# Eight heads' softmax weights and three groups of q and k in the second layer: transposed by VectorE and transfers instead of TensorE

## The chip, the cores and the metric

One core of a Trainium2 chip runs the whole kernel in one launch. The metric is the device time of that launch in microseconds (us). The runs of the kernel before took 2664.18 to 2666.12 us.

## The reference, cut to what matters

Two transformer layers work on 256 tokens of width 2048, in float32. Each layer has two attention mixers, A and B, that share one input projection, and then a gated feed-forward with a short convolution. Only mixer B's attention and the q and k that lead to it are touched:

```python
qb = rmsnorm(qb.reshape(B, S, HB, HEAD_DIM), qn_b[l])
kb = rmsnorm(kb.reshape(B, S, HB, HEAD_DIM), kn_b[l])
...
s = jnp.einsum('brqhd,brikhd->bhrqik', qg, kg) * (HEAD_DIM ** -0.5)
s = jnp.where(col_mask[None, None, None, :, None, :], s + bias[None], NEG_INF)
p = jax.nn.softmax(s.reshape(B, HB, rows, GRID_W, kh * GRID_W), axis=-1)
o = jnp.einsum('bhrqik,brikhd->brqhd', p, vg)
```

There are 8 heads of width 128 in each mixer. With 256 tokens the window of B spans all grid rows, so a head's scores and weights are a full 256x256 matrix with a bias that also masks.

## The kernel before

**Weights.** All weight matrices are cut into 128x128 blocks, laid out in the order of use and loaded in units of 16 blocks (1 MB) by SyncE (SP) into one of four `raw` buffers, which the `aw` blocks of the conditioning vector share. ScalarE (ACT) casts half a unit to the rounded type (line 297) and VectorE (DVE) subtracts to get the remainder (line 298); four such split halves (`hl`) can lie ready. TensorE (PE) multiplies with the high and low parts in three passes (lines 314 to 316 with features as the output rows, 377 to 379 with tokens).

**Order of work.** A scheduler orders the instructions of each engine by program order and readiness; every engine then runs its own queue in order. After each unit of weights `Stream.tick` runs the background: functions put off with `bg.defer` run at the next tick, and generators registered with a rate are advanced by that many steps per tick. The attention of a layer is such a generator, `attention`: each step advances every live head by one `yield` and starts a new head if its groups of q, k and v are ready (`ready`). Its rate in the second layer is 0.4 per tick (`ATT[1]`) from the third group's projection on, and `ATT_B[1]` (0.21) after mixer A's output projection. What is left when the gate of B has been computed is run at once (`bg.finish(job)`).

**The second layer.** After 8 rows of gate A come nine groups of 512 columns of q, k and v in token layout, four units each. Group 0 holds A's k and v, 1 and 2 its q; 3, 4, 5 are k, v, q of B's heads 0 to 3 and 6, 7, 8 the same for heads 4 to 7. Then follow the rest of gate A, A's projection, gate B and B's projection, which needs all heads of B.

**Turning q and k.** `qk_rows` squares and sums a group on ACT, takes the power -0.5 on GpSimd (POOL, line 441), norms it on DVE three ticks later (line 556), and one tick after that `turn` transposes it, head by head: 8 transposes on PE into PSUM (`qtp`, line 580) and two scalings by ACT back to SBUF (line 581).

**A head.** First step: the bias load (line 825) and the split of q and k. Second: scores on PE (`sc`, line 607), sum with the bias and maximum on DVE (line 610), exponential and division on ACT (lines 618, 626). Third: four transposes of the weights `p` on PE (`tp`, line 631), and their split into high and low parts on ACT and DVE (`pT`, lines 389, 390). Fourth: product with v (`po`, line 639) and the split of the result (`oB`, lines 641, 642).

GpSimd issues no transfer; its only work at this place is the small power of each group.

Of the kernel before, what the change touches and what calls it, by code (L numbers as in the profile page):

```python
# [26 lines left out]
EPS = 1e-6  # L27
NEG = -1e30
SCALE = HEAD ** -0.5
GRID_W, NA_KH, NA_KW = 64, 8, 16  # L30


QKV_GROUPS = [1024, 0, 512, 2560, 3584, 1536, 3072, 4096, 2048]
# [45 lines left out]
H_RATE = [2.7, 1.7]  # L79

ATT = [1.288, 0.4]
ATT_B = [0.21, 0.21]

SCORES_3 = (1,)

ADA_ORDER = [[p * KC + k for k in range(KC) for p in ps] for ps in ((0, 1), (2,), (3, 4), (5,))]
ADA_ORDER = [i for part in ADA_ORDER for i in part]
# [47 lines left out]
def encoder(ctx: ExitStack, tc: tile.TileContext, a: dict, out: bass.AP):  # L135
# [16 lines left out]
    sm = pool("sm", 3)  # L152
    mm = pool("mm", 4, space=bass.MemoryType.PSUM)
    ax = pool("ax", 3, space=bass.MemoryType.PSUM)

    ident = const.tile([P, P], F32, name="ident")
    make_identity(nc, ident[:])
# [118 lines left out]
                pass  # L276

    bg = Paced()

    def unit_steps(l, u, by_halves=False):  # L280

        raw = rawp.tile([P, UB * P], F32, name=f"w{l}_{u}", tag="raw")
        if not by_halves:
            nc.sync.dma_start(raw[:], a["ws"][l, u])
        halves = []
        streamed = any(m == "w_in" and mo < GATE_A // P for m, _, mo in STREAMS[l][u * UB : (u + 1) * UB])
        at = OFF if streamed else 0
        for j in range(2):  # L290
            n = UB * P // 2
            hl = hlp.tile([P, 2 * n + ROW], F32R, name=f"hl{l}_{u}_{j}", tag="hl")
            hl = hl[:, at : at + 2 * n].rearrange("p (a n) -> p a n", a=2)
            r = raw[:, j * n : (j + 1) * n]
            if by_halves:
                nc.sync.dma_start(r, a["ws"][l, u][:, j * n : (j + 1) * n])
            nc.scalar.copy(hl[:, 0], r)  # L297
            nc.vector.tensor_tensor(out=hl[:, 1], in0=r, in1=hl[:, 0].bitcast(F32), op=ALU.subtract)  # L298
            halves.append(hl)
            if j == 0:  # L300
                yield halves
# [234 lines left out]
            nc.vector.tensor_tensor(out=z[:], in0=ps[:, :S], in1=self.rbs[:], op=ALU.mult)  # L536
            return z, sh

    def qk_rows(pss, heads, rot, gain, dst, then):

        cols = 0
        n = heads * HEAD
        ss = sm.tile([P, 8], F32, name="qss", tag="qss")
        for t, ps in enumerate(pss):
            for i in range(heads):
                sq = at.tile([P, HEAD], F32, name="qsq", tag="qsq", bufs=1)
                nc.scalar.activation(
                    out=sq[:], in_=ps[:, cols + i * HEAD : cols + (i + 1) * HEAD], func=AF.Square,
                    accum_out=ss[:, t * heads + i : t * heads + i + 1],
                )  # L550
        rs = sm.tile([P, 8], F32, name="qrs", tag="qrs")
        rsqrt(rs[:, : 2 * heads], ss[:, : 2 * heads], HEAD, 2 * heads)
        def norm():
            qn = at.tile([P, 2, 4, HEAD], F32, name="qn", tag="qn", bufs=1)
            for t, ps in enumerate(pss):
                nc.vector.tensor_tensor(
                    out=qn[:, t, :heads],
                    in0=ps[:, cols : cols + n].rearrange("p (h d) -> p h d", d=HEAD),
                    in1=rs[:, t * heads : (t + 1) * heads].unsqueeze(2).broadcast_to([P, heads, HEAD]),
                    op=ALU.mult,  # L560
                )
            if rot is not None:
                x1, x2 = qn[:, :, :heads, :HALF], qn[:, :, :heads, HALF:ROT]
                tab = [rot[:, i].unsqueeze(2).broadcast_to([P, 2, heads, HALF]) for i in range(4)]
                tm = []
                for i in range(2):
                    z = ev.tile([P, S], F32, name=f"rt{i}", tag="z")
                    z = z[:].rearrange("p (i t h d) -> p i t h d", i=2, t=2, h=4)
                    tm += [z[:, 0, :, :heads], z[:, 1, :, :heads]]
                for i, src in enumerate((x1, x2, x2, x1)):  # L570
                    nc.vector.tensor_tensor(out=tm[i], in0=src, in1=tab[i], op=ALU.mult)
                nc.vector.tensor_tensor(out=x1, in0=tm[0], in1=tm[1], op=ALU.subtract)
                nc.vector.tensor_tensor(out=x2, in0=tm[2], in1=tm[3], op=ALU.add)
            bg.defer(lambda: turn(qn))

        def turn(qn):
            for t in range(2):
                ps = ax.tile([P, 4, P], F32, name="qtp", tag="ax")
                for h in range(heads):
                    nc.tensor.transpose(ps[:, h], qn[:, t, h], ident[:])  # L580
                nc.scalar.activation(
                    out=dst[:, :, t * P : (t + 1) * P], in_=ps[:, :heads], func=AF.Identity, scale=gain
                )
            then()

        bg.defer(lambda: bg.defer(lambda: bg.defer(norm)))
# [12 lines left out]

        return ((0, 0), (0, 1), (1, 0))[: 2 * len(x) - 1]  # L600

    def attend(q, k, v, p, mask, scale, sink, o):

        sc = ax.tile([P, 2, S], F32, name="sc", tag="ax")
        for t in range(2):
            for i, j in by(q):
                nc.tensor.matmul(sc[:, t], q[i][:, t * P : (t + 1) * P], k[j], start=i + j == 0, stop=(i, j) == by(q)[-1])  # L607
        m = sm.tile([P, 2], F32, name="m", tag="m")
        for t in range(2):
            nc.vector.tensor_tensor_reduce(  # L610
                out=p[:, t], in0=sc[:, t], in1=mask[:, t], scale=scale, scalar=-3.0e38 if sink is None else sink,
                op0=ALU.add, op1=ALU.max, accum_out=m[:, t : t + 1],
            )
        nm = sm.tile([P, 2], F32, name="nm", tag="nm")
        nc.vector.tensor_scalar(out=nm[:], in0=m[:], scalar1=-1.0, scalar2=None, op0=ALU.mult)
        den = sm.tile([P, 2], F32, name="den", tag="den")
        for t in range(2):
            nc.scalar.activation(out=p[:, t], in_=p[:, t], func=AF.Exp, bias=nm[:, t : t + 1], accum_out=den[:, t : t + 1])
        if sink is not None:
            es = sm.tile([P, 2], F32, name="es", tag="es")  # L620
            nc.scalar.activation(out=es[:], in_=nm[:], func=AF.Exp, bias=sink)
            nc.vector.tensor_tensor(out=den[:], in0=den[:], in1=es[:], op=ALU.add)
        ri = sm.tile([P, 2], F32, name="ri", tag="ri")
        nc.vector.reciprocal(out=ri[:], in_=den[:])
        for t in range(2):
            nc.scalar.activation(out=p[:, t], in_=p[:, t], func=AF.Copy, scale=ri[:, t : t + 1])
        yield
        tp = ax.tile([P, 2, S], F32, name="tp", tag="ax")
        for k in range(2):
            for t in range(2):  # L630
                nc.tensor.transpose(tp[:, k, t * P : (t + 1) * P], p[:, t, k * P : (k + 1) * P], ident[:])  # L631
        pT = at.tile([P, 2, 2, S], F32R, name="pT", tag="pT", bufs=1)
        split(pT, tp[:])
        v = v()
        yield
        po = ax.tile([P, 512], F32, name="po", tag="ax")
        for i, j in by(v):
            for b in range(2):
                nc.tensor.matmul(po[:, :S], v[i][:, b], pT[:, j, b], start=i + j + b == 0, stop=i + b == 2)  # L639
        o = o()  # L640
        nc.scalar.copy(o[:, 0], po[:, :S])
        nc.vector.tensor_tensor(out=o[:, 1], in0=po[:, :S], in1=o[:, 0].bitcast(F32), op=ALU.subtract)
# [115 lines left out]
    for l in range(L):  # L758
# [35 lines left out]
        kTa, qTa = packs[0][:, 0:3:2], packs[0][:, 4:12]  # L794
        kvs = [None, None]

        ready, heads = [0], [0]
        oA, oB = [], []

        def head_a(i):  # L800
# [15 lines left out]
                    kvs[1] = in_halves(packs[0][:, 1:4:2, g * HEAD : (g + 1) * HEAD], f"vA{l}_{g}", "vh", True)  # L816
                return kvs[1]

            yield from attend(q, k, v, p, tables[0], SCALE, sink[:, i : i + 1], lambda: oA[i])

        def head_b(hb):
            b, i = packs[1 + hb // 4], hb % 4
            v = b[:, 4:8].rearrange("p (t a) s -> p t (a s)", t=2)
            p = at.tile([P, 2, S], F32, name="p", tag="p")
            nc.sync.dma_start(p[:], a["bias"][l, hb])
            q = in_halves(b[:, 8 + i], f"qB{l}_{hb}", "qh", l in SCORES_3)
            k = in_halves(b[:, i], f"kB{l}_{hb}", "kh", l in SCORES_3)
            yield
            yield from attend(
                q, k, lambda: in_halves(v[:, :, i * HEAD : (i + 1) * HEAD], f"vB{l}_{hb}", "vh", True), p, p, 1.0, None,  # L830
                lambda: oB_of(hb),
            )

        def oB_of(hb):
# [36 lines left out]
        for pi, (groups, gates) in enumerate(parts):  # L871
            last = pi == len(parts) - 1
            for g, part in enumerate(groups):
# [14 lines left out]
                    continue  # L888

                def turned(g=g):  # L890
                    ready[0] = g + 1

                vcol = {0: GA * HEAD, 4: 0, 7: 0}.get(g)
                if vcol is not None and pi == 0:
# [4 lines left out]
                elif g < 3:  # L899
                    qk_rows(pss, 4, rots[0], gains[:, 0:1], dst, turned)  # L900
                elif vcol is None:
                    qk_rows(pss, 4, None, gains[:, 3:4] if g in (3, 6) else gains[:, 2:3], dst, turned)
                else:
                    turned()
                if g == 2:
# [243 lines left out]
```

## Time and profile before

| what | value |
|---|---|
| runs, device time | 2666.12, 2664.18, 2664.96 us; median 2664.96 |
| profiled execution | span 2663.2 us from the first to the last instruction; the median of the runs lies 1.8 us above it |
| PE busy | 2650.9 us, 100% of the span |
| DVE, ACT, POOL busy | 2102.2, 1412.8, 36.2 us (79%, 53%, 1%) |
| moved | 700.41 MB, mean 263 GB/s |
| granted clock of TensorE | 1.000 |

How to read it: matmuls overlap in the pipeline, so busy time of PE says that it had work, not how fast it went; the chain of work shows what each instruction costs on the path. In the answers below PEld is TensorE's weight load, SPq the queue of SP, "<-" behind an instruction names what it reads, and "x8" counts instructions.

### The profile page before, as it was taken

To read this page: it belongs to the slowest core of one execution; us is meant where nothing else is said; L and a number is where in the kernel's file an instruction comes from. 1 tells how busy PE (TensorE), PEld (TensorE's weight loads), DVE (VectorE), ACT (ScalarE), POOL (GpSimd) and SP (SyncE) were. 2 spreads that over 40 slices of the span, in tenths; PEclk is the share of its full clock that TensorE was granted. 3 is DMA by queue.
4 is the path that set the end of the run, shared out by engine and by line. 5 is a ranking of instruction groups with operands and counts; after the bars stand their busy time and mean duration, and the time that the engine had idled before them with its cause. 6 is when DMAs were issued, how large, how long until landed. Compare 5 with 4: busy or idle time off the path is not lost.

```text
span 2663.2 us, 50845 instructions
## 1 busy us (share of the span) xinstructions
PE 2650.9 (100%) x21256; PEld 2565.7 (96%) x21256; DVE 2102.2 (79%) x2959; ACT 1412.8 (53%) x2284; POOL 36.2 (1%) x25
## 2 busy tenths in 40 slices
PE   9999999999999999999999999999999999999999
PEld 7888899999999999999998889999999999999999
DVE  8898998997987888788976667768888866655664
ACT  5445865456644555355555566554565445544553
POOL 0001100000000000000000000000000000000000
PEclk9999999999999999999999999999999999999999
DMA  9987789885787878788766666666747765555554
GB/s 372 351 327 292 262 300 352 317 320 199 291 294 287 302 288 295 289 294 289 290 217 254 228 229 231 245 252 253 285 173 288 297 256 190 190 194 194 197 191 143
DMA packets 102039, 700.41 MB, mean 263 GB/s; under 512 B 12721, under 2 KB 15025, under 8 KB 17969
## 3 DMA queue, kind: packets, MB, share of 16 engines
q1 hardware_dynamic: 101810, 697.17, 71.4%
q8 instruction: 166, 2.72, 0.4%
q14 instruction: 63, 0.52, 0.1%
HBM read 695.03 MB, written 2.10 MB: 262 GB/s over the span
## 4 chain that ended last, share of the span: by engine, by line
PE 89%; DVE 6%; ACT 1%; issue 1%; DMA 1%; POOL 0%; SPq 0%; DVEq 0%; ACTq 0%
PE ps L314 25%; PE ps L316 25%; PE ps L315 25%; PE ps_t L377 4%; PE ps_t L379 4%; PE ps_t L378 4%; DVE hl L298 2%; DVE aw L226 2%; DMA aw<-in_aw 1%; PE sc L607 1%; PE po L639 1%; ACT hl L297 1%; PE tp L631 1%; POOL qrs L441 0%; PE qtp L580 0%
## 5 line engine op out<-in xcount | busy, mean ns | idle before, releaser
L298 DVE TENSOR_TENSOR hl<-w,hl 128x1024 fp32r<-128x1024 f32 x928 | 1128.3, 1222 | 360.0 <-ACT hl L297 357.6
L297 ACT CAST hl<-w 128x1024 fp32r<-128x1024 f32 x928 | 970.7, 1049 | 748.5 <-PE ps L316 518.1
L314 PE MATMUL ps<-h,hl 128*128 128x256 f32 x3328 | 922.8, 277 | 1.3 <-DVE ya L915 0.6
L315 PE MATMUL ps<-h,hl 128*128 128x256 f32 x3328 | 919.8, 276 | 0.0
L316 PE MATMUL ps<-h,hl 128*128 128x256 f32 x3328 | 919.8, 277 | 0.0
L314 PEld LDWEIGHTS ps<-h,hl 128*128 128x128 f32 x3328 | 624.8, 188 | 2.4 <-DVE ya L915 0.8
L315 PEld LDWEIGHTS ps<-h,hl 128*128 128x128 f32 x3328 | 625.3, 188 | 0.4 <-DVE h L470 0.2
L316 PEld LDWEIGHTS ps<-h,hl 128*128 128x128 f32 x3328 | 624.4, 188 | 0.0
L226 DVE CUSTOM_DVE_ANT_0 aw<-aw,cact,ab 128x2048 f32<-128x2048 f32 x189 | 443.5, 2347 | 48.8 <-DMA aw<-in_aw 47.8
L377 PE MATMUL ps_t<-hl,h 128*128 128x512 f32 x576 | 223.1, 392 | 2.6 <-ACT h L469 2.1
L378 PE MATMUL ps_t<-hl,h 128*128 128x512 f32 x576 | 224.9, 391 | 0.3
L379 PE MATMUL ps_t<-hl,h 128*128 128x512 f32 x576 | 224.3, 390 | 0.0
L994 DVE SCALAR_TENSOR_TENSOR u<-ps,cw,u 128x255 f32<-128x255 f32 x304 | 146.1, 481 | 66.5 <-ACT u L992 62.2
L992 ACT ACTIVATE u<-ps,cw 128x256 f32<-128x256 f32 x152 | 85.9, 565 | 187.9 <-PE ps L316 187.5
L316 PE MATMUL ps<-merged,hl 128*128 128x256 f32 x512 | 141.8, 277 | 0.4 <-DVE hl L298 0.4
L315 PE MATMUL ps<-merged,hl 128*128 128x256 f32 x512 | 141.6, 277 | 0.0
L314 PE MATMUL ps<-merged,hl 128*128 128x256 f32 x512 | 141.6, 277 | 0.0
L315 PE MATMUL ps<-act_o,hl 128*128 128x256 f32 x512 | 141.4, 276 | 0.0
L316 PE MATMUL ps<-act_o,hl 128*128 128x256 f32 x512 | 141.3, 276 | 0.0
L314 PE MATMUL ps<-act_o,hl 128*128 128x256 f32 x512 | 141.2, 276 | 0.0
L377 PEld LDWEIGHTS ps_t<-hl,h 128*128 128x128 f32 x576 | 107.9, 188 | 26.1 <-ACT h L469 3.1
L378 PEld LDWEIGHTS ps_t<-hl,h 128*128 128x128 f32 x576 | 108.1, 188 | 23.7 <-DVE hl L298 1.9
(231 smaller groups left out, 4612.5 us busy)
## 6 DMA issues: line engine op xcount, KB each, us to landing
w<-in_ws SPq DMA_DIRECT2D x463, 1024.0 KB, 4.9
aw<-in_aw SPq DMA_DIRECT2D x189, 1024.0 KB, 6.1
p<-in_bias SPq DMA_DIRECT2D x16, 256.0 KB, 4.2
x<-in_xT SPq DMA_DIRECT2D x4, 512.0 KB, 5.3
aw_o<-in_aw SPq DMA_DIRECT2D x2, 1024.0 KB, 12.3
out<-x SPq DMA_DIRECT2D x16, 128.0 KB, 2.1
w<-in_ws SPq DMA_DIRECT2D x2, 512.0 KB, 11.7
aw_b<-in_aw SPq DMA_DIRECT2D x1, 1024.0 KB, 18.1
```

Of the source, the lines that this page charges most:

```text
L226: nc.vector.tensor_tensor_reduce(out=raw[:], in0=raw[:], in1=cact[:], scale=1.0, scalar=ab[:, i : i + 1], op0=ALU.mult, op1=ALU.add, accum ...
L297: nc.scalar.copy(hl[:, 0], r)
L298: nc.vector.tensor_tensor(out=hl[:, 1], in0=r, in1=hl[:, 0].bitcast(F32), op=ALU.subtract)
L314: nc.tensor.matmul(out, hi, act[0], start=first, stop=False)
L315: nc.tensor.matmul(ps[:, :S], hi, act[1], start=False, stop=False)
L316: nc.tensor.matmul(out, lo, act[0], start=False, stop=last)
L377: nc.tensor.matmul(ps[:], xh, hi, start=kc == kcs[0], stop=False)
L378: nc.tensor.matmul(ps[:], xh, lo, start=False, stop=False)
L379: nc.tensor.matmul(ps[:], xl, hi, start=False, stop=kc == kcs[-1])
L607: nc.tensor.matmul(sc[:, t], q[i][:, t * P : (t + 1) * P], k[j], start=i + j == 0, stop=(i, j) == by(q)[-1])
L992: nc.scalar.activation(out=u, in_=ps, func=AF.Identity, scale=w[:, 1:2], bias=w[:, 3:4])
L994: nc.vector.scalar_tensor_tensor(out=u[:, to], in0=ps[:, of], scalar=w[:, j : j + 1], in1=u[:, to], op0=ALU.mult, op1=ALU.add)
```

## The change

In the second layer all eight heads of mixer B and the groups 3, 5 and 6 no longer use PE to transpose. `turned_blocks` lets DVE transpose a 128-row tile in blocks of 32x32 (for a head, two tiles of 256 columns, written over that head's q and k, which have been split by then; for a group, two of 512 columns). GpSimd then sends each band of 32 rows to a scratch tensor in HBM, its 128-byte pieces put at the block's place in the transposed matrix: four transfers per tile, eight per head or group. SP reads the result back, for a head in two transfers four ticks later, for a group in one transfer seven ticks later; each read-back also waits for the latest subtraction of weights on DVE (`halved`). A group's scaling follows two ticks after its read-back, on SBUF data, and the group counts as ready then; since groups may now get ready out of order, `ready` counts only an unbroken run. A moved head takes two more steps, and the rate after A's projection is 0.4 instead of 0.21. Mixer A (`MOVED`'s first numbers) and the first layer keep the transposes of PE; `BACK`'s first entry serves heads of A and is not used.

```diff
-ATT_B = [0.21, 0.21]
+ATT_B = [0.21, 0.4]
...
+BACK = [3, 4]
+MOVED_QK = [(), (3, 5, 6)]
+BACK_QK = 7
+MOVED = [(0, 0), (0, 8)]
...
+    dram = pool("dram", 2, space=bass.MemoryType.DRAM)
...
+    def read_back(dst, src):
+
+        tc.add_manual_dep(nc.sync.dma_start(dst, src).ins, halved[0], BEHIND)
...
+    def later(n, fn):
+
+        if n == 0:
+            fn()
+        else:
+            bg.defer(lambda: later(n - 1, fn))
+
+    def turned_blocks(p, rows, n, tag):
+
+        y = dram.tile([P, n, S], F32, name=tag, tag=tag)
+        to = y[:].rearrange("(b i) n (t a j) -> t a i n b j", i=BLOCK, t=2, a=P // BLOCK)
+        for t, row in enumerate(rows):
+            nc.vector.transpose(out=row, in_=p[t])
+            src = row.rearrange("p (n b j) -> p n b j", n=n, j=BLOCK)
+            for a in range(P // BLOCK):
+                nc.gpsimd.dma_start(to[t, a], src[a * BLOCK : (a + 1) * BLOCK])
+        return y
...
+            halved[0] = nc.vector.tensor_tensor(
+                out=hl[:, 1], in0=r, in1=hl[:, 0].bitcast(F32), op=ALU.subtract
+            ).ins.name
...
         def turn(qn):
+            if moved:
+                rows = dst.rearrange("p (t a) s -> p t (a s)", t=2)
+                y = turned_blocks(
+                    [qn[:, t].rearrange("p h d -> p (h d)") for t in range(2)], [rows[:, t] for t in range(2)], heads, "qY"
+                )
+
+                def scaled():
+                    nc.scalar.activation(out=dst, in_=dst, func=AF.Identity, scale=gain)
+                    then()
+
+                later(BACK_QK, lambda: read_back(dst, y[:]))
+                later(BACK_QK + 2, scaled)
+                return
...
+        if rows is not None:
+            rows = rows()
+            y = turned_blocks([p[:, t] for t in range(2)], rows, 2, "pY")
+
+            def back():
+                for k in range(2):
+                    read_back(rows[k], y[:, k])
+
+            back = once(back)
+            later(BACK[sink is None], back)
+            yield
+            yield
+            back()
+            pT = at.tile([P, 2, 2, S], F32R, name="pT", tag="pT", bufs=1)
+            for k in range(2):
+                split(pT[:, :, k], rows[k])
+        else:
...
                 def turned(g=g):
-                    ready[0] = g + 1
+                    through.add(g)
+                    while ready[0] in through:
+                        ready[0] += 1
...
-                lambda: oB_of(hb),
+                lambda: oB_of(hb), (lambda: [b[:, 8 + i], b[:, i]]) if hb < MOVED[l][1] else None,
```

More of the change, by code (lines that the diff above doesn't have):

```diff
@@ L29 @@
 SCALE = HEAD ** -0.5
+BEHIND = mybir.DependencyInfo(mybir.DependencyClass.Sync, mybir.DependencyReason.DATA)
 GRID_W, NA_KH, NA_KW = 64, 8, 16
+BLOCK = 32
 QKV_GROUPS = [1024, 0, 512, 2560, 3584, 1536, 3072, 4096, 2048]
@@ L278, in encoder, with once, run @@
     bg = Paced()
+    halved = [None]
+    def once(fn):
+        due = [fn]
+        def run():
+            if due:
+                due.pop()()
+        return run
+    def read_back(dst, src):
[14 more added lines that the diff above has]
+        return y
     def unit_steps(l, u, by_halves=False):
@@ L297, in unit_steps @@
             nc.scalar.copy(hl[:, 0], r)
-            nc.vector.tensor_tensor(out=hl[:, 1], in0=r, in1=hl[:, 0].bitcast(F32), op=ALU.subtract)
+            halved[0] = nc.vector.tensor_tensor(
+                out=hl[:, 1], in0=r, in1=hl[:, 0].bitcast(F32), op=ALU.subtract
+            ).ins.name
             halves.append(hl)
@@ L537, in level, with qk_rows @@
             return z, sh
-    def qk_rows(pss, heads, rot, gain, dst, then):
+    def qk_rows(pss, heads, rot, gain, dst, then, moved=False):
         cols = 0
@@ L600, in by, with attend @@
         return ((0, 0), (0, 1), (1, 0))[: 2 * len(x) - 1]
-    def attend(q, k, v, p, mask, scale, sink, o):
+    def attend(q, k, v, p, mask, scale, sink, o, rows=None):
         sc = ax.tile([P, 2, S], F32, name="sc", tag="ax")
@@ L627, in attend @@
         yield
[L628 to L633, printed above, removed]
+        if rows is not None:
[13 more added lines that the diff above has]
+        else:
+            tp = ax.tile([P, 2, S], F32, name="tp", tag="ax")
+            for k in range(2):
+                for t in range(2):
+                    nc.tensor.transpose(tp[:, k, t * P : (t + 1) * P], p[:, t, k * P : (k + 1) * P], ident[:])
+            pT = at.tile([P, 2, 2, S], F32R, name="pT", tag="pT", bufs=1)
+            split(pT, tp[:])
         v = v()
@@ L795, in encoder @@
         kvs = [None, None]
-        ready, heads = [0], [0]
+        ready, heads, through = [0], [0], set()
         oA, oB = [], []
@@ L817, in v, with rows @@
                 return kvs[1]
-            yield from attend(q, k, v, p, tables[0], SCALE, sink[:, i : i + 1], lambda: oA[i])
+            def rows():
+                spare = ev.tile([P, S], F32, name=f"spare{l}_{i}", tag="r", bufs=2)
+                return [qTa[:, i], spare[:]]
+            yield from attend(
+                q, k, v, p, tables[0], SCALE, sink[:, i : i + 1], lambda: oA[i], rows if i < MOVED[l][0] else None
+            )
         def head_b(hb):
@@ L901, in encoder @@
                 elif vcol is None:
-                    qk_rows(pss, 4, None, gains[:, 3:4] if g in (3, 6) else gains[:, 2:3], dst, turned)
+                    qk_rows(pss, 4, None, gains[:, 3:4] if g in (3, 6) else gains[:, 2:3], dst, turned, g in MOVED_QK[l])
                 else:
```

## The prediction

> **What bounds the kernel now.** I read the page's totals first, then its chain of work, then the stage in question in 50 us windows.
>
> ```profile
> span 2663.2 us, 50845 instructions
> ...
> PE 2650.9 (100%) x21256; PEld 2565.7 (96%) x21256; DVE 2102.2 (79%) x2959; ACT 1412.8 (53%) x2284; POOL 36.2 (1%) x25
> ...
> PE 89%; DVE 6%; ACT 1%; issue 1%; DMA 1%; POOL 0%; SPq 0%; DVEq 0%; ACTq 0%
> ```
>
> TensorE carries 89% of the chain. The page is an average over the launch, so the windows (columns: length, then busy time of PE, PEld, DVE, ACT and POOL, clock, DMA share, GB/s) show the second layer's attention: up to about 1600 us the 512-column matmuls of q, k, v (245 in 50 us), then the 256-column ones of gates and projections (440).
>
> ```profile
> 1500.00:1550.00 50.00, 50.00 (x245) 42.10 (x244) 34.13 (x54) 32.00 (x65) 1.64 (x1) 1.00 0.63 229
> 1550.00:1600.00 50.00, 50.00 (x249) 42.26 (x248) 33.01 (x56) 31.61 (x70) 1.64 (x1) 1.00 0.62 231
> 1650.00:1700.00 50.00, 50.00 (x438) 50.00 (x438) 37.52 (x70) 28.27 (x52) 0.00 (x0) 1.00 0.64 235
> 1700.00:1750.00 50.00, 50.00 (x441) 50.00 (x440) 34.34 (x51) 28.10 (x53) 0.00 (x0) 1.00 0.65 242
> ...
> L607 PE MATMUL sc<-kB,qB x48: 276/276/369, 1633.8 to 1767.6; 128*128 128x256 f32 x48
> L631 PE MATMUL tp<-ident,p x128: 270/272/331, 281.1 to 1796.0; 128*128 128x128 f32 x128
> ```
>
> The last two rows, from the views of the tiles `sc` and `tp`, date the heads of B: first scores at 1633.8, last transposes at 1796.
>
> PE is busy throughout at clock 1.00. The view of waits, PE alone, from 1400 to 1830 us has one row:
>
> ```profile
> PE ps L315 <- DVE oB L642: 0.3, 1, 0.3
> ```
>
> So here each microsecond of PE work is one of wall time, DVE has 12 to 17 us free in 50, ACT 18 to 22, the transfer engines over a third, and POOL is nearly empty. Work taken from PE shortens this stage one for one, as long as its substitute never holds up the weights.
>
> **Removed: transposes on PE.** The chain in order of time (start, length) gives their price on the path.
>
> ```profile
> 1646.11 0.44 PE tp L631 x4
> ...
> 1694.92 0.70 PE po L639 x6
> 1695.62 0.44 PE tp L631 x4
> 1696.06 0.70 PE sc L607 x6
> ...
> 1556.48 0.87 PE qtp L580 x8
> ...
> 1581.04 0.87 PE qtp L580 x8
> ```
>
> Each head of mixer B loses four `tp`, 0.44 us; eight heads: 3.5 us. Groups 3, 5, 6 lose eight `qtp` each, 0.87 us; three groups: 2.6 us. Sum 6.1 us, which is 0.23% of 2663.2. That is the whole gain to be had here, because PE's waits in the stage add up to 0.3 us. Nothing in the first layer changes, and no other matmul goes; with those 0.3 the stage can give 6.4.
>
> **Added on DVE and ACT, under cover.** A transposition in blocks does not occur in the trace. Its nearest rows are elementwise operations of the same size:
>
> ```profile
> L390 DVE TENSOR_TENSOR pT<-tp,pT 128x512 fp32r<-128x512 f32 x16 | 10.9, 682 | 0.1
> L610 DVE CUSTOM_DVE_ANT_0 p<-sc,p 128x256 f32<-128x256 f32 x16 | 6.1, 418 | 0.0
> ...
> L581 ACT ACTIVATE packB<-qtp,gains x16: 667/690/696, 287.3 to 1633.1; 128x512 f32<-128x512 f32 x16
> ```
>
> DVE gains 16 of 128x256 at 0.42 us (6.7) and 6 of 128x512 at 0.68 (4.1); each `pT` split becomes two of 256 columns, 0.84 for 0.68, so 1.3 more over eight heads. Sum 12 us over the 250 us from 1545 to 1795, where the windows leave DVE at least 60 free. Even at four times the price a head's two blocks cost 3.4 us in a beat of 15 and fit. ACT trades two scalings of 512 columns (1.38 us) for one of 1024 (about the 1.05 of a weight cast below). I take nothing for these, covered by DVE's and ACT's idle time; bare of cover they would cost 12 us. Fewer gaps on DVE could also bring up to 0.3, the PE wait above.
>
> **Added on POOL: the unknown price.** Per head 2 x 4 transfers of 32 KB, cut into 256 pieces of 128 bytes; per group 8 of 64 KB in 512 pieces. That is 64 + 24 = 88 transfers. POOL issues none before, so the price `c` of one in POOL's queue must be bounded:
>
> ```profile
> 1562.91 1.64 POOL L441 TENSOR_TENSOR qrs<-qss,mhalf 128x8 f32<-128x8 f32 x1 [26.63 <-DVE qss L440]
> ...
> 1646.58 0.33 SPq L825 DMA_DIRECT2D p<-in_bias  x1
> 1648.07 0.33 SPq L286 DMA_DIRECT2D w<-in_ws  x1
> ...
> p<-in_bias SPq DMA_DIRECT2D x16, 256.0 KB, 4.2
> ```
>
> Low end 0.33 us, what SP needs to issue one. High end 4.2 us, the landing of the bias (256 rows of 1 KB, the same number of pieces), if every transfer had to wait for the one before. I take 1.64, POOL's time for a tiny instruction: the only row of that engine. It is nearest because eight transfers of a head are independent and may overlap.
>
> [...]
>
> **What c must not exceed.** The attention steps run at 0.4 per tick (one tick is one 1 MB unit of weights). These starts of `po` already stand at that rate, before the slower 0.21 sets in; with 1694.92 above, two beats:
>
> ```profile
> 1663.67 0.70 PE po L639 x6
> ...
> 1676.53 0.70 PE po L639 x6
> ```
>
> (1694.92 - 1663.67) / 2 = 15.6 us a head, 6.2 us a tick. At c = 1.64 a head's eight transfers take 13.1 us and POOL keeps up. The read-back is put off four ticks, 25 us. It stands in SP's queue, and every load of weights, `aw` and bias behind it waits with it. How long may it be late?
>
> ```profile
> L297 ACT CAST hl<-w x572: 1030/1050/1062, 16.8 to 1658.5; 128x1024 fp32r<-128x1024 f32 x191
> L286 SPq DMA_DIRECT2D w<-in_ws x287: 327/328/1261, 9.3 to 1648.1; - x144
> L296 SPq DMA_DIRECT2D w<-in_ws x2: 328/402/476, 5.3 to 9.0; - x2
> ...
> 1668.29 1.06 ACT L297 CAST hl<-w 128x1024 fp32r<-128x1024 f32 x1 [1.85 <-PE ps L316]
> 1689.44 1.06 ACT L297 CAST hl<-w 128x1024 fp32r<-128x1024 f32 x1 [1.70 <-PE ps L316]
> 1692.20 1.06 ACT L297 CAST hl<-w 128x1024 fp32r<-128x1024 f32 x1 [1.70 <-PE ps L316]
> ...
> w<-in_ws SPq DMA_DIRECT2D x463, 1024.0 KB, 4.9
> ...
> L298 DVE TENSOR_TENSOR hl<-w,hl 128x1024 fp32r<-128x1024 f32 x134 | 163.1, 1223 | 101.3 <-ACT hl L297 101.0
> ```
>
> Up to 1660 us SP has issued 287 units and one more in two halves, 288 in all, the last at 1648.07. The casts so far are 572 halves, so unit 288 is cast as number 575, the third after 1660, at 1668.29: 20.2 us after issue, 15.3 after a 4.9 us landing. Behind that four split halves lie ready, 2.76 us of PE each (1692.20 - 1689.44), less one cast and one subtraction (2.3): 8.7 us. PE thus notices a loading delay only after about 24 us.
>
> The eighth head's transfers end 64c after the first head's blocks; its read-back is due 7 x 15.6 + 25 = 134 us after them, and 24 more are hidden. POOL costs nothing up to c = 158 / 64 = 2.5 us. For the groups, 5 and 6 come closest, 24.6 us apart (1556.48 and 1581.04), with seven ticks, 43 us, of delay: 16c' = 24.6 + 43 + 24 gives c' = 5.7. Readiness comes nine ticks later, for group 5 at 1556.5 + 9 x 6.2 = 1612 and for group 6 at 1637; the first head of B starts its scores at 1634 and needs only groups 3 to 5, its fifth the rest.
>
> POOL's queue has another customer: each group's power `qrs`, and DVE stands still behind it.
>
> ```profile
> 1536.31 1.29 DVE L556 TENSOR_TENSOR qn<-ps_t,qrs 128x512 f32<-128x512 f32 x2 [1.81 <-POOL qrs L441]
> ```
>
> Group 5 is normed at 1536.3, its blocks can follow one tick later, 1542.5, and group 6's power comes at 1562.9: 20.4 us for eight transfers, so DVE waits from c' = 2.5 on, and behind it all halvings; PE has 8.7 us in hand, so it pays from c' = 3.6.
>
> **Added on the transfer engines and SP.** 64 x 256 + 24 x 512 = 28,700 short packets, 16 read-backs of 128 KB and three of 512 KB. The end of the kernel, where little but the 1 KB rows of `out` moves, bounds a short packet:
>
> ```profile
> 2640.00:2650.00 10.00, 10.00 (x90) 10.00 (x90) 4.86 (x7) 4.21 (x4) 0.00 (x0) 1.00 0.09 28
> ```
>
> 0.09 x 16 x 10 us over 273 packets is 53 ns. By bytes alone an eighth, 7 ns. So 12 to 95 us on each of 16 engines, spread over 250 us: share 0.64 becomes 0.69 to 1.0. I take a value near the low end, by bytes, and no loss; at the high end landings lengthen into the 24 us. 19 issues of 0.33 us cost SP nothing.
>
> **Sum.** 2663.2 - 6.1 = 2657.1 us of span. The median of 2664.96 lies 1.8 above the profiled span; that stays: 2658.9, forecast **2659.0**, if it holds 2657 to 2660.
>
> **Rivals.** (1) *The gain is eaten.* Group 6's power waits behind group 5's transfers, or a split waits some microseconds for its read-back behind 1 MB loads: PE loses 1 to 7 us, once or twice. At c' = 4, for instance, 32 - 20.4 - 8.7 = 3 us: 2662. For it: DVE already waits for POOL 1.8 us a group. Against: the slacks above.
>
> (2) *POOL becomes the bound, slower.* Place: SP's queue at the read-backs of the last heads. It decides from c = 2.5 us. At c = 3, which lies between my value and the high end, 64 x 3 - 158 = 34 us: 2693; at 4.2, 111 us: 2770. For it: transfers of many pieces written by an engine whose smallest instruction takes 1.64 us. Against: the same row, if pieces cost little.
>
> [...]
>
> **How the numbers follow.** Forecast 0.42, (1) 0.26, (2) 0.28, (3) 0.04. What a measurement can tell from no change is about 0.2%, 5.3 us: faster means below 2659.6, and the full gain clears that by less than 1 us. Faster 0.42, same 0.26, slower 0.32. The range starts at 2656.5, the forecast less the 0.3 of idle and 2 us for an altered order elsewhere, and goes to 2685, c = 2.9, leaving out (3) and about half of (2).
>
> **What would show it.** Right: PE loses 56 matmuls and the waits of PE stay under 1 us from 1500 to 1800; POOL shows under 2 us per transfer; casts of weights wait for PE, not for transfers. Wrong: casts `hl` waiting for `w`, read-backs on SP waiting long for POOL, DVE waiting for `qrs` over 9 us, or DVE's blocks costing far over 0.7 us.

## The result and the profile after

The changed kernel takes 2661.87 us (median of 18 runs, 2658.79 to 2665.32), the kernel before 2665.14 in the same comparison: ratio 0.9986, 95% interval 0.998 to 0.9993, so 1.9 to 5.3 us are saved, 3.7 by the ratio. The forecast was 6.1 us. The profiled run of the changed kernel has a span of 2661.6 us. Its page, totals, queues and chain:

```profile
span 2661.6 us, 50990 instructions
...
PE 2646.2 (99%) x21200; PEld 2560.0 (96%) x21200; DVE 2108.9 (79%) x2989; ACT 1411.9 (53%) x2289; POOL 94.4 (4%) x113
...
q0 software_dynamic: 2816, 3.68, 0.5%
...
PE 85%; DVE 7%; ACT 2%; DMA 2%; issue 2%; POOL 1%; SPq 0%; ACTq 0%; DVEq 0%; POOLq 0%
```

PE has exactly 56 matmuls fewer, POOL 88 instructions more, and a new queue, that of GpSimd's transfers, has appeared. Spans mix the change with the first layer, which varies from run to run (the second layer's first power starts at 1420.17 before and 1422.05 after, though nothing ahead of it differs). I therefore compare a stage: from that power to the power of the second layer's feed-forward norm. It holds all that was moved. First and last row of POOL's timeline (start, length), before, then after:

```profile
1420.17 1.05 POOL L441 TENSOR_TENSOR qrs<-qss,mhalf 128x4 f32<-128x4 f32 x1 [65.82 <-DVE qss L440]
...
1938.96 0.70 POOL L457 TENSOR_TENSOR nrs<-nss,mhalf 128x2 f32<-128x2 f32 x1 [323.97 <-DVE nss L519]
```

```profile
1422.05 1.05 POOL L484 TENSOR_TENSOR qrs<-qss,mhalf 128x4 f32<-128x4 f32 x1 [65.80 <-DVE qss L483]
...
1937.52 0.71 POOL L500 TENSOR_TENSOR nrs<-nss,mhalf 128x2 f32<-128x2 f32 x1 [180.69 <-DVE nss L562]
```

518.79 us became 515.47: 3.3 us less, about what the launch shows. The windows of the changed kernel and PE's waits from 1400 to 1830 us say where the rest went:

```profile
1550.00:1600.00 50.00, 48.43 (x235) 40.29 (x234) 36.08 (x60) 28.68 (x66) 9.91 (x13) 1.00 0.70 239
1600.00:1650.00 50.00, 48.76 (x392) 47.12 (x392) 34.04 (x59) 34.04 (x75) 6.83 (x9) 1.00 0.67 243
1650.00:1700.00 50.00, 50.00 (x439) 50.00 (x438) 39.95 (x80) 28.06 (x52) 14.71 (x24) 1.00 0.88 304
...
PE ps_t L421 <- DVE hl L339: 1.6, 1, 1.6
PE ps L359 <- DVE hl L339: 1.2, 1, 1.2
```

PE now stands still twice for a split half of weights, 2.8 us in all, and both times while groups of q and k are on their way, not while the heads are (1650 to 1700 is full). 6.1 - 2.8 = 3.3, which is what is missing. (The rate, measured below, is worth another 0.6 us that this sum leaves out, so it closes to about half a microsecond.) The first pause can be followed back through three engines, POOL first, then DVE, then PE:

```profile
1540.80 0.78 POOL L318 DMA_DIRECT2D qY<-packB  x1 [3.49 <-DVE packB L315]
1543.47 0.75 POOL L318 DMA_DIRECT2D qY<-packB  x1 [1.89 <-issue]
...
1564.10 0.74 POOL L318 DMA_DIRECT2D qY<-packB  x1 [3.69 <-issue]
1568.31 0.75 POOL L318 DMA_DIRECT2D qY<-packB  x1 [3.46 <-issue]
1569.07 1.67 POOL L484 TENSOR_TENSOR qrs<-qss,mhalf 128x8 f32<-128x8 f32 x1
...
1564.00 0.17 DVE L483 TENSOR_SCALAR qss<-qss 128x8 f32<-128x8 f32 x1
1570.77 1.29 DVE L599 TENSOR_TENSOR qn<-ps_t,qrs 128x512 f32<-128x512 f32 x2 [6.60 <-POOL qrs L484]
...
1573.11 1.30 DVE L315 STREAM_TRANSPOSE packB<-qn 128x512 f32<-128x512 f32 x2
1574.33 2.31 DVE L234 CUSTOM_DVE_ANT_0 aw<-aw,cact,ab 128x2048 f32<-128x2048 f32 x1
...
1576.57 1.22 DVE L339 TENSOR_TENSOR hl<-w,hl 128x1024 fp32r<-128x1024 f32 x1
...
1577.84 0.50 PE L421 MATMUL ps_t<-hl,h 128*128 128x512 f32 x1 [1.56 <-DVE hl L339]
```

Group 5's eight transfers take POOL from 1540.8 to 1569.1, 28.3 us, though each is only 0.75 us of work; between them POOL waits, mostly for something that the profile calls "issue". Group 6's sums are there at 1564.2, but its power stands behind the last transfer. DVE waits 6.6 us for it (1.8 before), and the halvings of weights stand behind it. DVE then does one halving, the group's blocks and an `aw` before the halving of 1576.57, and that is the one PE has run out for.

### The profile page after: what moved, and what is told of

The parts are those of the page before. It is cut to its first block, busy times and chain, and to the rows that moved or that the text cites. A ratio compares the mean times of both kernels' runs of the same rounds, so it can differ in the third digit from the quotient of the medians.

```text
span 2661.6 us, 50990 instructions
## 1 busy us (share of the span) xinstructions
PE 2646.2 (99%) x21200; PEld 2560.0 (96%) x21200; DVE 2108.9 (79%) x2989; ACT 1411.9 (53%) x2289; POOL 94.4 (4%) x113
## 3 DMA queue, kind: packets, MB, share of 16 engines
q0 software_dynamic: 2816, 3.68, 0.5%
## 4 chain that ended last, share of the span: by engine, by line
PE 85%; DVE 7%; ACT 2%; DMA 2%; issue 2%; POOL 1%; SPq 0%; ACTq 0%; DVEq 0%; POOLq 0%
PE ps L357 25%; PE ps L359 25%; PE ps L358 25%; PE ps_t L422 3%; PE ps_t L420 3%; PE ps_t L421 3%; DVE hl L339 3%; DVE aw L234 2%; DMA aw<-in_aw 2%; ACT hl L338 1%; PE sc L663 1%; PE po L712 1%; ACT qsq L590 0%; POOL qrs L484 0%; DMA packB<-qY 0%
```

## The experiments

**My theory.** The transposes taken off PE are worth 6.1 us; the loss comes from POOL's queue, where the transfers of a group are strung out because only so many of their pieces fit at a time into the scratch that GpSimd has for transfers (`dynamic_dma_scratch_size`, in bytes; not the scratch tensor in HBM); a second, smaller loss from the loads that stand behind group 6's read-back on SP. **Rivals:** the heads' traffic costs something; the transfers are slow to prepare; the read-backs hold up the weights.

**Parts alone.** Only heads: `MOVED_QK = [(), ()]`.

> Heads of mixer B moved as in the changed kernel, no groups of q and k moved. Stage = from the start of the second layer's first power qrs to the start of the power nrs of its feed-forward norm: 518.8 us before (1420.17 to 1938.96), 515.5 changed (1422.05 to 1937.52). Theory 1: the heads give their full 8 x 0.44 = 3.5 us and the 2.8 us lost on TensorE come from the groups alone: stage 515.3, no TensorE wait on hl between 1400 and 1830, launch about 3.5 us under before. Rival: the heads' transfers (DMA share 0.88 in 1650 to 1700 against 0.64) cost something too: stage 516.5 to 518.

Stage 514.55 (4.24 less, and 0.75 less than expected), no wait of PE at all, ratio 0.9978 (0.9969 to 0.9987). The heads give their share and lose nothing. Only groups: `MOVED = [(0, 0), (0, 0)]`, `ATT_B = [0.21, 0.21]`.

> Groups 3, 5 and 6 moved, no heads, the rate after A's projection back at 0.21. Theory 1: 2.6 us saved and 2.8 us lost in two waits of TensorE on hl (behind the power of group 6, and behind the aw load that stands behind group 6's read-back): stage 518.8 to 519, launch as before within 1 us. Rival: the losses need the heads as well: stage 516.2, launch 2.6 us under before.

Stage 518.49, just under what I expected, PE waits of 1.7 on `hl` and 0.3 on `oB` (the latter stood there before), ratio 0.9997 (0.9989 to 1.0006): moving the three groups at this scratch is worth nothing that can be measured. Here PE paid only at the second place; at the first, DVE waited 5.1 us and PE had just enough in hand. Only the rate: both lists empty, `ATT_B = [0.21, 0.4]`.

> Nothing is moved; only the rate of the attention after A's projection is 0.4 instead of 0.21. Theory 1: the rate brings at most the 0.3 us of TensorE's wait for oB: stage 518.4 to 518.8, launch as before. Rival (a part of the 4.2 us that the moved heads alone saved came from the rate): stage 517.5 to 518.2.

Stage 518.23, ratio 0.9998 (0.9989 to 1.0006). By this one profile the rate is worth 0.56 us in the stage, about twice the wait of 0.3 that I had named and at the edge of the rival's range; 4.24 - 0.56 = 3.7 remain for eight heads, against 3.5. Stages of single profiles fit such sums only to about half a microsecond, so the 0.56 is rough.

**The power behind the transfers.** Group 5 stays on PE: `MOVED_QK = [(), (3, 6)]`.

> As changed, but group 5 is left on TensorE, so that no power comes behind a group's transfers within 30 us. Theory 1: saves 3.5 + 2 x 0.87 = 5.2 us; VectorE's longest wait for qrs falls from 6.6 to 1.8 us, TensorE's wait of 1.6 us near 1578 is gone; the one of 1.2 us near 1634 may stay: stage 513.6 to 514.8. Rival (the loss belongs to the read-backs and to transfers in general, not to the power): stage 515.5 to 516.4, with 1 to 2 us of TensorE waits left.

Stage 513.50, DVE's longest wait for `qrs` 1.8 us, PE's pause near 1578 gone and 0.5 us left at the second place; ratio 0.9981 (0.9972 to 0.999). It saves less PE work than the changed kernel, yet its stage is 2 us shorter than in the profile above. Two more profiles with group 5 moved, below, have 513.64 and 513.95, so most of those 2 us is spread between runs; what this run shows is that DVE's long wait and PE's first pause go with group 5's transfers.

**Room for pieces.** More scratch, with 512 bytes freed elsewhere; the order of instructions on every engine is that of the changed kernel:

```diff
-    nc = _bacc.Bacc("TRN2", target_bir_lowering=False, num_devices=1, dynamic_dma_scratch_size=1024)
+    nc = _bacc.Bacc("TRN2", target_bir_lowering=False, num_devices=1, dynamic_dma_scratch_size=1536)
...
-                sq = at.tile([P, HEAD], F32, name="qsq", tag="qsq", bufs=1)
+                sq = ev.tile([P, HEAD], F32, name="qsq", tag="sqa", bufs=1)
```

> As changed, with 1536 instead of 1024 bytes of scratch for GpSimd's transfers; the 512 bytes come from the squares' junk output, which now lies in another buffer. The order of instructions is the same. Theory 1: POOL's pauses between transfers (2 to 5.5 us between two of a group, three of a head in a row and then a pause) are waits for room for their pieces: two of a group and five of a head fit now, a group's eight take under 20 us instead of 28, VectorE's longest wait for qrs falls from 6.6 to about 2 us, and TensorE's wait behind it is gone: stage 513.9. Rival: the pauses are the time of preparing the pieces: a group keeps 28 us, stage 515.5.

> The kernel with 1536 bytes of scratch once more. Theory 1: stage 512.5 to 513.2, TensorE's waits under 0.7 us, launch 1 to 3 us under the changed kernel in the same comparison, about 6 us under before. Rival (its first result was the chip's): no difference to the changed kernel.

Stages 512.77 and 512.78, PE waits 0.6 and 0.8, ratios 0.9971 (0.996 to 0.9983) and 0.997 (0.9959 to 0.9981). The stages are 1.1 us below the 513.9 that I expected of the first; the 0.8 lies just above my 0.7. POOL's timeline of the first of these runs, with group 5 and the first head:

```profile
1538.02 1.52 POOL L318 DMA_DIRECT2D qY<-packB  x2 [3.49 <-DVE packB L315]
1540.70 1.51 POOL L318 DMA_DIRECT2D qY<-packB  x2 [1.16 <-issue]
...
1551.66 0.74 POOL L318 DMA_DIRECT2D qY<-packB  x1 [2.69 <-issue]
1561.31 1.67 POOL L484 TENSOR_TENSOR qrs<-qss,mhalf 128x8 f32<-128x8 f32 x1 [8.91 <-DVE qss L483]
...
1637.65 3.06 POOL L318 DMA_DIRECT2D pY<-packB  x5 [26.25 <-DVE packB L315]
1640.96 1.82 POOL L318 DMA_DIRECT2D pY<-packB  x3 [0.25 <-issue]
```

Two of a group go at once instead of one, five of a head instead of three; the eight are through in 14.4 us (1538.02 to 1552.40), and POOL is idle when the power comes. The same first head with 1024 and with 768 bytes:

```profile
1643.14 1.86 POOL L318 DMA_DIRECT2D pY<-packB  x3 [25.39 <-DVE packB L315]
1646.82 1.86 POOL L318 DMA_DIRECT2D pY<-packB  x3 [1.82 <-issue]
```

```profile
1644.04 1.26 POOL L318 DMA_DIRECT2D pY<-packB  x2 [26.50 <-DVE packB L315]
1646.99 1.23 POOL L318 DMA_DIRECT2D pY<-packB  x2 [1.69 <-issue]
```

With 256 pieces a transfer, 2, 3 and 5 in a row at 768, 1024 and 1536 bytes, and one or two of 512 pieces at 1024 and 1536: the pieces under way stay below the number of bytes, and one transfer more would reach it. Counted over the whole of the changed kernel, from each issue to its landing, the pieces under way peak at 768; with 768 bytes no row of transfers is longer than two, 512 pieces. And in the changed kernel each of group 5's transfers starts 0.3 us after the one before has landed, whether that took 2.3 or 5.5 us. That is room as the limit, and not the preparing. Two controls. Only the output of the squares that nobody reads (`qsq`, the junk output) moved as above, scratch 1024:

> As changed with scratch at 1024, and only the squares' junk output moved to the other buffer as in the run with more scratch. Theory 1: the move does nothing by itself; stage 515 to 516, VectorE's longest wait for qrs near 6.6 us, POOL's group chains 28 us. Rival (the gain of that run came from the other place of the buffers): stage 512.8, launch as in that run.

Launch ratio 0.9988 (0.9979 to 0.9997), as the changed kernel, and DVE's wait for `qrs` still 5.0 us. The stage of the profiled run was 513.64, lower than I expected of it. And the changed kernel again:

> The changed kernel once more, beside the next one. Theory 1: the launch lies about 3 us under before; in the profiled run TensorE's waits on hl between 1400 and 1830 add up to 1 to 3 us and the stage is 512.5 plus these waits, 513.5 to 515.5. Rival (the profiled run of the changed kernel was an odd one): waits under 0.5 us and a launch 6 us under before.

Ratio 0.9984 (0.9975 to 0.9992); stage 513.95 with 1.8 us of PE waits. So the profiled run of the changed kernel was on the high side, by 1.5 us. With DVE at the edge, how long POOL's transfers take to land decides from run to run whether PE notices: group 5's eight took 28.3 us there, 26.8 in the repeat and with the junk output moved, 26.4 with the groups alone; DVE then waited 6.6, 5.2, 5.0 and 5.1 us, and PE's first pause was 1.6, 0.4, 0.5 and none. The three profiles with all moved and 1024 bytes have stages of 513.6 to 515.5, the two with 1536 both 512.8. The launches' intervals overlap, so the gain of scratch on the launch, some 2 to 4 us, is likely rather than proven.

A way without more scratch: each transfer of a group in two of 16 rows.

```diff
-                nc.gpsimd.dma_start(to[t, a], src[a * BLOCK : (a + 1) * BLOCK])
+                step = 2 * BLOCK // n
+                for i in range(0, BLOCK, step):
+                    nc.gpsimd.dma_start(to[t, a][i : i + step], src[a * BLOCK + i : a * BLOCK + i + step])
```

> As changed, scratch at 1024, but each transfer of a group goes in two of 16 rows: 16 transfers of 256 pieces instead of 8 of 512, like those of the heads. Theory 1 (POOL waits for room for pieces): three of the small ones fit where one large one did, so that one and a half times as much is under way: a group's chain falls from 28 to about 19 us, VectorE's longest wait for qrs to about 2 us, stage 513 to 513.9. Rival (each transfer costs POOL a fixed time of preparation): 16 transfers take longer than 8, over 28 us, VectorE's wait grows beyond 6.6 us, stage 516 to 518.

Stage 513.05, group 5's sixteen transfers through in 19.6 us (1542.63 to 1562.23), DVE's longest wait for `qrs` 1.9, PE's waits 1.0, ratio 0.9978 (0.9969 to 0.9987). Twice as many transfers are faster, which speaks against a price per transfer.

**Less room.** `dynamic_dma_scratch_size=768`, the same order of instructions.

> As changed, with 768 bytes of scratch instead of 1024: two transfers of a head fit at a time instead of three, one of a group as before. Theory 1 (room for pieces sets POOL's pace): a head's eight transfers take about 17 us at 4.3 us of landing each, over the 15.6 of a beat, POOL falls behind from head to head, SP's waits for pY at the read-backs rise from 4 us to 10 us and more, and the stage grows by 0 to 5 us to 515 to 520. Rival (POOL has room to spare): SP's waits and the stage stay as in the changed kernel, 513.5 to 515.5.

Slower: ratio 1.0012 (1.0004 to 1.0021), stage 521.74, more than I allowed. Waits of this kernel, SP, DVE, PE:

```profile
SPq L301 <- DMA pY<-packB: 56.7, 23, 7.2
...
DVE aw L234 <- DMA aw<-in_aw: 38.0, 13, 6.5
...
PE ps L359 <- DVE hl L339: 7.0, 6, 3.5
```

This is rival (2) of the prediction, at its place: the read-backs wait on SP for POOL, the loads behind them are late, and PE pays: some 6 of the 7.0 us fall between 1728 and 1798, where the heads' read-backs are. The 64 transfers of the heads ran from 1644.04 to 1780.88, 2.1 us each with all pauses (the changed kernel: 114 us, 1.8).

**No extra wait at the read-back.** `read_back` without the dependence on `halved`, only `nc.sync.dma_start(dst, src)`.

> As changed, but the read-backs no longer wait for the latest subtraction on VectorE; in SP's order they stand one to three loads earlier. Theory 1: SP then waits for POOL's transfers at the read-backs (now 5.5 us in all), by 20 us and more in all, hidden up to about 24 us each: TensorE loses 0 to 5 us more, stage 515.5 to 520. Rival (the extra wait itself holds back the loads of aw behind it, and is what costs 1.2 us near 1634): stage 513 to 515.

Far worse than either theory: ratio 1.0144 (1.013 to 1.0158), stage 557.2. With nothing to hold them back, the scheduler's order lets SP come to the read-backs, and ACT to the scalings that use them, long before POOL's transfers have landed. SP waits 123 us at them; what PE feels is ACT's row, 44.0 us, because ACT's casts of weights queue behind it:

```profile
SPq L301 <- DMA pY<-packB: 71.1, 26, 9.4
...
SPq L301 <- DMA qY<-packB: 52.0, 11, 12.2
...
ACT packB L627 <- DMA packB<-qY: 44.0, 3, 16.2
...
PE ps_t L420 <- ACT hl L338: 22.2, 3, 9.3
```

Three windows of the same run (the last three numbers of a row are the granted clock, the DMA share and GB/s):

```profile
1570.00:1580.00 10.00, 6.55 (x37) 5.56 (x35) 0.00 (x0) 0.00 (x0) 2.23 (x3) 0.97 0.14 21
1580.00:1590.00 10.00, 3.68 (x8) 2.62 (x9) 2.31 (x4) 6.47 (x15) 1.67 (x1) 0.52 0.41 158
1590.00:1600.00 10.00, 7.49 (x33) 5.75 (x32) 10.00 (x17) 3.09 (x8) 1.53 (x2) 1.00 0.59 205
```

PE stood still for 9.3 us, into the second window; the eight matmuls behind the pause share 3.68 us of busy time there, 0.46 each, at a granted clock of 0.52, the 33 of the third window 7.49, 0.23 each, at 1.00. So this pause cost more than itself. Shorter pauses were not alike: the third window has 2.5 us without work for PE, and the ten us behind it show 0.83, while the run with 768 bytes, whose longest wait of PE for a split half was 3.5 us, has a mean clock of 1.000 (this run 0.993). The pauses of 1.6 and 1.2 us in the changed kernel lie in windows of 1.00.

**More of the same.** The kernel with 1536 bytes and six heads of mixer A moved as well, `MOVED = [(0, 0), (6, 8)]`.

> As the run with 1536 bytes of scratch (stage 512.8), with the softmax weights of the first six heads of mixer A in the second layer moved as well. Theory 1: each head more takes 0.44 to 0.53 us off TensorE: 2.6 to 3.2 us, stage 509.6 to 510.2, if POOL gets through three groups at 14 us and six heads at 10 us, about 100 us of work in the 115 us from 1495 to 1610. Rival: the powers now stand behind the heads' transfers, VectorE waits for qrs over 10 us at a time and the halvings behind it come late: stage 513 to 518.

The rival came, and by far more than its 513 to 518: ratio 1.0042 (1.003 to 1.0055), stage 529.6. Among PE's waits are 6.5 us for a split half and 5.4 for the softmax weights of a head that stayed on PE; DVE's row shows why:

```profile
1573.68 1.29 DVE L599 TENSOR_TENSOR qn<-ps_t,qrs 128x512 f32<-128x512 f32 x2 [11.47 <-POOL qrs L484]
```

POOL had groups and heads at once, and the power stood behind both. PE's pauses of 6.5 and 5.4 us lie in the windows 1550 to 1600 and 1600 to 1650, whose granted clock was 0.93 each, against 1.00 in those before and behind, which adds to the loss.

## Why the prediction was right, and where it was not

*What is saved* held: 6.1 us. The heads gave 3.7; the groups 0.3 net of 1.7 us of new waits; with enough scratch the stage fell by 6.0 with under 1 us of waits left, the rate's 0.56 included.

*DVE's and the transfer engines' part* held: after the change the blocks are one row each,

```profile
L315 DVE STREAM_TRANSPOSE packB<-p 128x256 f32<-128x256 f32 x16 | 6.4, 430 | 1.7 <-ACT p L682 1.7
L315 DVE STREAM_TRANSPOSE packB<-qn 128x512 f32<-128x512 f32 x6 | 3.9, 687 | 0.0
```

6.4 and 3.9 us against 6.7 and 4.1. The new queue holds 0.5% of 16 engines' span, 13 us each, at the low end of 12 to 95; it records 32 packets a transfer, as many as a band has rows, not 256 or 512.

*POOL's price* was the mis-sized term. I took 1.64 us for both kinds. The heads cost about 1.1 us each when POOL had one head (8.5 us for the first eight) and 1.8 over all; a group's transfer costs 28.3 / 8 = 3.5 us. Only one of 512 pieces was under way, so each paid its landing, 2.3 to 5.5 us in group 5. That no row before showed a limit on what POOL may have under way is why I bounded `c` by 4.2 but took a value that assumed overlap. The 1.64 was also read badly: I called it the only row of POOL and its smallest instruction, but the 0.70 and 1.05 us shown above stood in the same trace, and the instruction of a transfer takes 0.61 or 0.75. The price was the wait between transfers, which no row of a POOL instruction could give.

*The queue behind POOL* was named with its place: 8c' - 20.4 gives a wait of 7.6 us at 3.5, and 6.6 was measured, of which 1.7 is the power itself. But I let PE pay only from c' = 3.6, with 8.7 us in hand; it paid 1.6 us at 3.5, and in the other profiles it began to pay at a DVE wait of about 5 us. The 8.7 took off only one cast and one subtraction, and put the rest that DVE has to do between two halvings, here the norm, the blocks and an `aw` (1.29 + 1.30 + 2.31 us), at nothing. So the likeliest case, no loss, did not come; rival (1) did. That it said 2662 and 2661.9 was measured is partly luck: its 3 us were one pause at c' = 4, and the 2.8 here are two pauses at 3.5, the second from another cause. And a range from 2656.5 to 2685 would have held most outcomes.

*The slack* of 24 us was too generous, as the run with 768 bytes shows: at 136.8 us for the 64 transfers my formula, 64c - 158, is still 21 us below zero, and PE already lost 7.0 us to split halves. I had measured how late a load of weights may come. But `aw` loads queue behind the read-backs as well, and DVE, which must halve the weights, stands still at the first `aw` that is late (38 us there, 18 in the changed kernel, 8 before).

*The 0.04 of (3)* stood for a price of 6.6 us a transfer, four times mine, because of a busy DVE. No run shows such a term: the 64 head transfers took POOL 612 to 642 ns each, nearly all of them in windows (1650 to 1750) in which DVE was 79 and 80% busy.

*Left open:* the second pause, 0.5 to 1.7 us near 1630 (the 1634 of the expectations). It is in the profiled runs of the changed kernel, its repeat, more scratch, half transfers, the junk output, group 5 kept on PE and the groups alone, all of which move group 6; it is absent with the heads alone and with the rate alone, which do not. The chain runs from the late `aw` to the read-back ahead of it; taking away only that read-back's extra wait was not possible without moving the rest, as the run without the dependence shows.

## What to carry to other kernels

Moving work off a full engine paid one for one here only while its substitute's queue had room (the heads 3.7 us for 3.5 taken off, the groups 0.3 for 2.6): look for who else uses that queue (here a power of 1.6 us that VectorE waits for) and give the order of arrival there as much care as the amount. GpSimd's fine-grained transfers were limited here by how many pieces fit in its scratch, so enlarge the scratch, or cut transfers so that several fit, before judging such an idea; here more scratch took the ratio from 0.9986 to 0.997, the best version run, though the intervals still touch. Slack must be computed for the first thing that stops in a shared queue, not for the one that matters most, and with everything else that engine has to do in the same time.

## What the hardware showed that I had not expected

GpSimd's queue stopped for room: behind 2, 3 and 5 transfers of 256 pieces at 768, 1024 and 1536 bytes of scratch, while the instruction itself took 0.61 us (0.75 for 512 pieces). In the changed kernel transfers of 32 and 64 KB landed in 4.8 and 4.1 us (median; 1.9 to 7.2 and 2.3 to 6.4) beside the stream of weights. And a pause of TensorE of 9.3 us was followed by about half its granted clock (0.52 in the 10 us shown); stretches of 50 us with pauses of 6.5 and 5.4 us had 0.93.
